# Sums of squares of the queries as rows in column tiles, turned to columns through DRAM

## The chip, the cores and the metric

The kernel runs on one core of a Trainium2 chip. A core has TensorE (PE) for matrix products, VectorE (DVE), ScalarE (ACT) and GpSimd (POOL) for elementwise work, SyncE (SP) that here only issues DMAs, and sixteen DMA engines. Each engine takes its instructions from its own queue in order, and semaphores connect the queues. The metric is the device time of one execution in microseconds.

## The reference

One layer of a streaming encoder is computed for 256 prompt rows and 64 sample rows together, so 320 time steps. After a projection, queries and keys are normalised per head, attention runs over bands of chunks, a gating part runs beside it, both are projected back, and a feed-forward part follows. What matters here is the normalisation of the queries:

```python
def rmsnorm(x, g):
    xf = x.astype(jnp.float32)
    y = xf * lax.rsqrt(jnp.mean(xf * xf, axis=-1, keepdims=True) + EPS)
    return (y * g.astype(jnp.float32)).astype(x.dtype)

z = rmsnorm(x, ln_g) @ w_in
q = z[..., :ATTN_WIDTH].reshape(*lead, N_KV_HEADS, GQA_GROUP, HEAD_DIM)
...
return rmsnorm(q, q_g), rmsnorm(k, k_g), v, zs
...
s = jnp.einsum('...qhgd,...khd->...hgqk', q, k).astype(jnp.float32) * (HEAD_DIM ** -0.5) + bias
```

There are 16 query heads of 64 values. For each head and time step one number is needed, the reciprocal root of the sum of 64 squares. It does not have to be multiplied into the query; it can be applied to the row of scores that the query gives.

## The kernel before, in words

Activations lie transposed: features on the 128 partitions, the 320 time steps along the free axis. Two heads fill the 128 partitions of one feature tile. A projection (`product`, `products`) makes 256 output features at a time, from 16 contraction tiles in four pieces of four. Each piece loads 512 KB of weights (`w_raw`, issued by SP), splits them into a high part on ACT (`w_hi`, line 115) and a low part on DVE (`w_lo`, line 116), three buffers of each, and PE runs 24 matmuls on them: high by high, high by low, low by high for eight products (line 141). All projections of the program follow one another on PE like this. Small work is put between pieces by `between_pieces`; its PE instructions go directly behind the last matmul of that piece.

The queries are made in four groups g of four heads (two feature tiles a, two heads p in each). `evict_q` scales a group, stores it in `qT` as [feature, block b of 64 steps, tile, step], and ACT squares it into `qsq`. `norm_q` (from line 316) then sums the squares. It uses the squares themselves as the stationary operand: for each of five blocks, 128 columns (two tiles of 64 steps) against `hone`, two columns of ones over the upper and lower 64 partitions. So the result stands as columns: partition = tile and step, two numbers per block, ten per group. DVE adds the epsilon (`r_q`, line 324) and GpSimd raises to the power -0.5 (`rq`, line 325). `rq` is read in `scores` (line 426) as a per-partition scalar when DVE takes a unit's scores out of PSUM.

The four calls stand behind pieces: group 0 in the first piece of the third query projection, group 1 in its third, group 2 in the second piece of the fourth projection, group 3 in the third piece of the first projection of v. Attention unit 0 (`attend(0)`, whose score matmuls are line 415) follows group 2; units 0 to 4 read `rq` of groups 0 and 1, units 5 to 9 that of groups 2 and 3. The scores also need `kzv`, the keys laid out in two halves, which DVE fills and two DMAs on GpSimd's queue complete (lines 371 and 372). The order within each engine's queue is set by the framework's scheduler, from the program's order and an estimate of times.

Of the kernel before, what the change touches and what calls it, by code (L numbers as in the profile page):

```python
# [8 lines left out]
F32 = mybir.dt.float32  # L9
F32R = mybir.dt.float32r  # L10
I32 = mybir.dt.int32
AF = mybir.ActivationFunctionType
ALU = mybir.AluOpType
AX = mybir.AxisListType

P = 128
T = 320
# [6 lines left out]
EPS = 1e-6  # L24
GELU_A = 0.044715
GELU_S = 0.7978845608028654
HD = 64
# [3 lines left out]
def hymba_step_kernel(ctx: ExitStack, tc: tile.TileContext, i, o):  # L31
    nc = tc.nc

    const = ctx.enter_context(tc.tile_pool(name="const", bufs=1))
    actp = ctx.enter_context(tc.tile_pool(name="actp", bufs=2))
    wp = ctx.enter_context(tc.tile_pool(name="wp", bufs=3))
    sm = ctx.enter_context(tc.tile_pool(name="sm", bufs=2))
    phase1 = ExitStack()
    at = phase1.enter_context(tc.tile_pool(name="at", bufs=2))
    dram = ctx.enter_context(tc.tile_pool(name="dram", bufs=1, space=bass.MemoryType.DRAM))  # L40
# [34 lines left out]

    ident = const.tile([P, P], F32, name="ident")
    make_identity(nc, ident)
    nhalf = const.tile([P, 16], F32, name="nhalf")
    nc.vector.memset(nhalf, -0.5)
    warm = const.tile([P, 1], F32, name="warm")  # L80
    nc.scalar.activation(out=warm, in_=nhalf[:, 0:1], func=AF.Exp)
# [12 lines left out]
    nc.gpsimd.memset(mean_hd.bitcast(F32), 0.0)  # L94
    for h in range(2):
        nc.gpsimd.memset(mean_hd[h * HD:(h + 1) * HD, h * HD:(h + 1) * HD].bitcast(F32), 1.0 / HD)
    hone = const.tile([P, 2], F32, name="hone")
    nc.vector.memset(hone, 0.0)
    nc.vector.memset(hone[0:HD, 0:1], 1.0)
    nc.vector.memset(hone[HD:P, 1:2], 1.0)  # L100
# [196 lines left out]
        nc.scalar.activation(out=kv, in_=kv_ps[:, :, 0:T], func=AF.Copy)  # L297
    rk, rx = rstd_b("rk"), rstd_b("rx")

    rq = at.tile([P, 4, 10], F32, name="rq", bufs=1)  # L300

    def evict_q(g, q_ps):
        qg = qT[:, :, 2 * g:2 * g + 2]
# [10 lines left out]
        nc.scalar.activation(out=sq, in_=qg, func=AF.Square)  # L314
        return sq

    def norm_q(g, sq):
        st = misc()
        for b in range(5):
            mm = nc.tensor.matmul(out=st[:, 2 * b:2 * b + 2], lhsT=sq[:, b].rearrange("p a t -> p (a t)"), rhs=hone,  # L320
                                  start=True, stop=True)
        narrow.append(mm.ins)
        r = at.tile([P, 10], F32, name="r_q", tag="r_q")
        nc.vector.tensor_scalar(out=r, in0=st[:, 0:10], scalar1=HD * EPS, scalar2=None, op0=ALU.add)
        nc.gpsimd.tensor_tensor(out=rq[:, g], in0=r, in1=nhalf[:, 0:10], op=ALU.pow)

# [27 lines left out]
    q0_sq = evict_q(0, q0_ps)  # L356
    q0_out = rests[-1]
    q1_sq = []

    def first_norms():  # L360
        rstd(ksq, mean_hd, EPS, rk)
        norm_q(0, q0_sq)
        q1_sq.append(evict_q(1, q1_ps))

    def keys():
        for dst, c in ((kn[:, 0:256], slice(0, 256)), (kn[:, 384:448], slice(256, 320))):
            nc.vector.scalar_tensor_tensor(out=dst, in0=zk[:, c], scalar=g_k, in1=rk[:, c], op0=ALU.mult, op1=ALU.mult)
        for h in range(2):
            hs = slice(h * HD, (h + 1) * HD)
            nc.vector.tensor_scalar(out=kz[hs, h], in0=kn[hs], scalar1=g_q[hs], scalar2=None, op0=ALU.mult)  # L370
        nc.gpsimd.dma_start(out=kz[HD:P, 0], in_=kz[0:HD, 0])
        nc.gpsimd.dma_start(out=kz[0:HD, 1], in_=kz[HD:P, 1])
        nc.gpsimd.dma_start(out=o["kpT"], in_=kn[:, 128:256])
        nc.gpsimd.dma_start(out=o["ksT"], in_=kn[:, 384:448])
        nc.gpsimd.dma_start(out=o["vpT"], in_=vT[:, 128:256])
        nc.gpsimd.dma_start(out=o["vsT"], in_=vT[:, 256:320])
        norm_q(1, q1_sq[0])
        values(0, 1)

    q2_ps = product(w_in, 0, KT, 512, xh, xl,  # L380
                    between_pieces={0: first_norms, 2: keys, 3: lambda: values(2, 3, 4, 5)},
                    halves_behind={1: lambda: q0_out})
    q2_sq = evict_q(2, q2_ps)

# [21 lines left out]
    def scores(u):  # L406
        blk_, kv = units[u]
        q0, k0, nk, b0 = blocks[blk_][0:4]
        js = slice(2 * kv, 2 * kv + 2)
        s_ps = [score_bank(p) for p in range(2)]  # L410
        for j in range(2):
            a = 2 * (2 * kv + j)
            for p in range(2):
                hs = slice(p * HD, (p + 1) * HD)
                mm = nc.tensor.matmul(out=s_ps[p][:, j * nk:(j + 1) * nk],  # L415
                                      lhsT=qT[hs, blk_, a:a + 2].rearrange("p a t -> p (a t)"),
                                      rhs=kz[hs, kv, k0:k0 + nk], start=True, stop=True)
        last = mm
        s = at.tile([P, 2, 2, 192], F32, name="s", tag="s", bufs=2)

        sv = s[:, :, :, 0:nk] if nk > HD else \
            s.rearrange("x p j k -> x p (j k)")[:, :, P:2 * P].rearrange("x p (j k) -> x p j k", j=2)
        for p in range(2):
            for j in range(2):
                c = 2 * blk_ + p
                nc.vector.scalar_tensor_tensor(out=sv[:, p, j], in0=s_ps[p][:, j * nk:(j + 1) * nk],
                                               scalar=rq[:, 2 * kv + j, c:c + 1],
                                               in1=bias[:, p, 2 * kv + j, b0:b0 + nk], op0=ALU.mult, op1=ALU.add)
        m = at.tile([P, 2, 2], F32, name="m", tag="m")
        nc.vector.tensor_reduce(out=m, in_=sv, axis=AX.X, op=ALU.max)  # L430
        sk = sinks_pj[:, :, js]
        nc.vector.tensor_tensor(out=m, in0=m, in1=sk, op=ALU.max)
        nm = at.tile([P, 2, 2], F32, name="nm", tag="nm")
        nc.vector.tensor_scalar(out=nm, in0=m, scalar1=-1.0, scalar2=None, op0=ALU.mult)
        es = at.tile([P, 2, 2], F32, name="es", tag="es")
        nc.vector.tensor_tensor(out=es, in0=sk, in1=m, op=ALU.subtract)
        nc.scalar.activation(out=es, in_=es, func=AF.Exp)
        den = at.tile([P, 2, 2], F32, name="den", tag="den")
        for p in range(2):
            for j in range(2):  # L440
                nc.scalar.activation(out=sv[:, p, j], in_=sv[:, p, j], func=AF.Exp, bias=nm[:, p, j:j + 1],
                                     accum_out=den[:, p, j:j + 1])
        nc.vector.tensor_tensor(out=den, in0=den, in1=es, op=ALU.add)
        nc.vector.reciprocal(out=den, in_=den)
        nc.gpsimd.tensor_tensor(out=sv, in0=sv,
                                in1=den[:, :, :, None].to_broadcast([P, 2, 2, nk]), op=ALU.mult)
        probs[u] = s
        return last

    def attend(i):  # L450
# [34 lines left out]
        if t is not None:  # L485
            for p in range(2):
                c = slice(min(x for _, x in cols) * P, (max(x for _, x in cols) + 1) * P)
                nc.vector.tensor_copy(out=pts[t % 2][p][:, c], in_=bank[p][:, c])

    q3_ps = product(w_in, 0, KT, 768, xh, xl,  # L490
                    between_pieces={1: lambda: (norm_q(2, q2_sq), attend(0)), 3: lambda: attend(1)})
    q3_sq = evict_q(3, q3_ps)

    def add_square(acc, src, first):
# [24 lines left out]
    acc_v = sums_rows("acc_v")  # L519
    for g in range(4):  # L520
        v_ps = product(w_in, 0, KT, 2304 + g * 256, xh, xl, between_pieces={
            1: lambda: attend(2 * g + 2), 2: lambda: norm_q(3, q3_sq) if g == 0 else None,
            3: lambda: attend(2 * g + 3)})
        gelu2(v_ps, gv[:, 2 * g:2 * g + 2])
        for a in range(2 * g, 2 * g + 2):
            add_square(acc_v, gv[:, a], a == 0)
            nc.gpsimd.tensor_scalar(out=gv[:, a], in0=gv[:, a], scalar1=g_sv[:, a:a + 1], scalar2=None, op0=ALU.mult)
# [195 lines left out]
```

## Time and profile before

| what | value |
|---|---|
| median of 3 runs | 1246.65 us (1246.59 to 1246.72) |
| span of the profiled execution | 1245.0 us |
| PE busy | 1240.9 us |
| DVE, ACT, POOL busy | 656.2, 491.3, 97.3 us |
| granted TensorE clock | 1.000 |
| DMA, mean | 151 GB/s |

The profiled execution's own time outside the profiler is not recorded; its span, first to last instruction, is 1.65 us below the median. In timeline rows the columns are start, length, engine, line, operation, output and inputs by the program's names, the tile of the array that a matmul uses (rows*columns), shape, and count of merged instructions; a bracket gives idle time before and what ended it. A plain fp32 matmul appears as two records, one for each pass.

### The profile page before, as it was taken

How to read it: one execution, taken by the hardware profiler on the slowest of the kernel's cores; microseconds unless marked ns; L12 is line 12 of the kernel's file. 1: busy time of each engine (PE TensorE's matmuls, PEld its weight loads, DVE VectorE, ACT ScalarE, POOL GpSimd, SP SyncE). 2: the span in 40 equal slices, each digit the busy share in tenths (PEclk: the TensorE clock that was granted, in tenths of full speed). 3: DMA queues.
4: the chain of work that ended last, by engine and by line, in shares of the span. 5: the costliest groups of instructions: out<-in, count | busy, mean ns of one | idle time of the engine just before them, and what ended most of it. 6: DMA issues, size and time to landing. Idle time of an engine off the chain costs nothing.

```text
span 1245.0 us, 20317 instructions
## 1 busy us (share of the span) xinstructions
PE 1240.9 (100%) x8560; PEld 1231.7 (99%) x8560; DVE 656.2 (53%) x787; ACT 491.3 (39%) x651; POOL 97.3 (8%) x89
## 2 busy tenths in 40 slices
PE   9999999999999999999999999999999999999998
PEld 9999999999999999999999999999999999999998
DVE  7777775987864444334454434444443344444343
ACT  7435655424543333333343333333333223433321
POOL 1134462201200000000000000000000000000000
PEclk9999999999999999999999999999999999999999
DMA  9744344544444444444444444445444444545540
GB/s 281 211 140 119 106 118 146 189 146 152 151 148 146 150 151 152 153 148 147 148 150 152 153 153 143 149 149 152 153 153 150 142 149 152 153 152 163 168 164 33
DMA packets 186988, 187.86 MB, mean 151 GB/s; under 512 B 6656, under 2 KB 186432, under 8 KB 186896
## 3 DMA queue, kind: packets, MB, share of 16 engines
q1 hardware_dynamic: 186096, 185.38, 48.0%
q8 instruction: 67, 1.10, 0.4%
q0 software_dynamic: 368, 0.93, 0.2%
q10 hardware_dynamic: 432, 0.24, 0.1%
q14 instruction: 25, 0.20, 0.0%
HBM read 182.98 MB, written 3.32 MB: 150 GB/s over the span
## 4 chain that ended last, share of the span: by engine, by line
PE 100%; DVE 0%; DVEq 0%; issue 0%
PE acc L141 93%; PE q_ps L237 1%; PE acc L237 1%; PE misc L141 1%; PE s_ps L415 1%; PE misc L465 0%; PE misc L472 0%; PE misc L320 0%; PE misc L84 0%; PE misc L538 0%; PE misc L477 0%; PE g_ps L551 0%; PE misc L551 0%; PE misc L186 0%; PE misc L187 0%; PE g_ps L553 0%
## 5 line engine op out<-in xcount | busy, mean ns | idle before, releaser
L116 DVE TENSOR_TENSOR w_lo<-w_raw,w_hi 128x1024 fp32r<-128x1024 f32 x332 | 413.3, 1245 | 430.5 <-ACT w_hi L115 422.0
L115 ACT ACTIVATE w_hi<-w_raw 128x1024 fp32r<-128x1024 f32 x332 | 351.8, 1060 | 697.6 <-PE acc L141 660.3
L141 PE MATMUL acc<-H2H,w_hi 128*128 128x320 f32 x1024 | 316.4, 309 | 0.0
L141 PE MATMUL acc<-H2L,w_hi 128*128 128x320 f32 x1024 | 316.4, 309 | 0.0
L141 PE MATMUL acc<-H2H,w_lo 128*128 128x320 f32 x1024 | 316.4, 309 | 0.0
L141 PE MATMUL acc<-FH,w_hi 128*128 128x320 f32 x992 | 306.5, 309 | 0.0
L141 PE MATMUL acc<-FL,w_hi 128*128 128x320 f32 x992 | 306.5, 309 | 0.0
L141 PE MATMUL acc<-FH,w_lo 128*128 128x320 f32 x992 | 306.5, 309 | 0.0
L141 PEld LDWEIGHTS acc<-H2H,w_lo 128*128 128x128 f32 x1024 | 192.2, 188 | 0.0
L141 PEld LDWEIGHTS acc<-H2H,w_hi 128*128 128x128 f32 x1024 | 192.2, 188 | 0.0
L141 PEld LDWEIGHTS acc<-H2L,w_hi 128*128 128x128 f32 x1024 | 192.2, 188 | 0.0
L141 PEld LDWEIGHTS acc<-FH,w_hi 128*128 128x128 f32 x992 | 186.2, 188 | 0.0
L141 PEld LDWEIGHTS acc<-FL,w_hi 128*128 128x128 f32 x992 | 186.2, 188 | 0.0
L141 PEld LDWEIGHTS acc<-FH,w_lo 128*128 128x128 f32 x992 | 186.2, 188 | 0.0
L141 PE MATMUL acc<-XH,w_hi 128*128 128x320 f32 x352 | 110.8, 315 | 0.0
L141 PE MATMUL acc<-XH,w_lo 128*128 128x320 f32 x352 | 108.8, 309 | 0.0
L141 PE MATMUL acc<-XL,w_hi 128*128 128x320 f32 x352 | 108.7, 309 | 0.0
L141 PEld LDWEIGHTS acc<-XH,w_hi 128*128 128x128 f32 x352 | 66.1, 188 | 2.1 <-issue 1.2
L141 PEld LDWEIGHTS acc<-XL,w_hi 128*128 128x128 f32 x352 | 66.1, 188 | 0.0
L141 PEld LDWEIGHTS acc<-XH,w_lo 128*128 128x128 f32 x352 | 66.1, 188 | 0.0
L639 DVE SCALAR_TENSOR_TENSOR tf<-acc,r 128x640 f32<-128x640 f32 x32 | 26.4, 825 | 41.9 <-PE acc L141 41.8
L654 DVE TENSOR_TENSOR xT<-xT,acc 128x640 f32<-128x640 f32 x31 | 25.5, 821 | 41.8 <-PE acc L141 41.8
(221 smaller groups left out, 1060.5 us busy)
## 6 DMA issues: line engine op xcount, KB each, us to landing
w_raw<-in_w_up SPq DMA_DIRECT2D x128, 512.0 KB
w_raw<-in_w_down SPq DMA_DIRECT2D x128, 512.0 KB
w_raw<-in_w_in SPq DMA_DIRECT2D x44, 512.0 KB
w_raw<-in_w_out SPq DMA_DIRECT2D x32, 512.0 KB
w_first<-in_w_in SPq DMA_DIRECT2D x14, 256.0 KB
out_yT<-xT SPq DMA_DIRECT2D x7, 320.0 KB
xT<-in_xT SPq DMA_DIRECT2D x8, 160.0 KB
xT<-in_xT SPq DMA_DIRECT2D x4, 320.0 KB
```

What stands on the lines that cost most here:

```text
L115: return (pin(nc.scalar.activation(out=hi, in_=raw, func=AF.Copy)).ins, pin(nc.vector.tensor_tensor(out=lo, in0=raw, in1=hi.bitcast(F32), ...
L116: pin(nc.vector.tensor_tensor(out=lo, in0=raw, in1=hi.bitcast(F32), op=ALU.subtract)).ins)
L141: mm = nc.tensor.matmul(out=out, lhsT=w_[:, k, g * P:(g + 1) * P], rhs=r_(kk), start=(kk == 0 and x == 0), stop=(kk == nk - 1 and x == 2))
L237: mm = nc.tensor.matmul(out=ps[:, 0:T], lhsT=w_[:, j, k, g * P:(g + 1) * P], rhs=r_(a + k), start=(a + k == 0 and x == 0), stop=(a + k == ...
L415: mm = nc.tensor.matmul(out=s_ps[p][:, j * nk:(j + 1) * nk], lhsT=qT[hs, blk_, a:a + 2].rearrange("p a t -> p (a t)"), rhs=kz[hs, kv, k0:k ...
L639: nc.vector.scalar_tensor_tensor(out=t, in0=ps[:, :, 0:T], scalar=0.0, in1=r2[:, None, :].to_broadcast([P, 2, T]), op0=ALU.max, op1=ALU.mult)
L654: nc.vector.tensor_tensor(out=xT[:, a, c], in0=xT[:, a, c], in1=p, op=ALU.add)
```

## The change

`norm_q` now takes two groups at once. The stationary operand is `hone`, widened to 32 columns with ones in the first two and zeros in the rest, and the squares stream past it: for each of four feature tiles c (two groups, two tiles) one fp32 matmul of 320 columns writes 32 partitions of one PSUM bank, from partition 32c on. Two rows of each 32 carry sums. ACT copies the bank to SBUF (`q_rows`), four DMAs on GpSimd's queue write the two rows of each tile into a DRAM tensor `q_dram`, and two DMAs read them back so that 64 time steps stand on partitions, with 20 numbers each (two heads, two groups, five blocks). DVE adds the epsilon in place, GpSimd takes the power of 20 columns. `scores` finds its column through `r_at`. The first call moves behind the second piece of the third query projection and covers groups 0 and 1; the second replaces the call of group 3 and covers groups 2 and 3.

```diff
-    nhalf = const.tile([P, 16], F32, name="nhalf")
+    nhalf = const.tile([P, 20], F32, name="nhalf")
...
-    hone = const.tile([P, 2], F32, name="hone")
+    hone = const.tile([P, 32], F32, name="hone")
...
-    rq = at.tile([P, 4, 10], F32, name="rq", bufs=1)
+    rq = at.tile([P, 40], F32, name="rq", bufs=1)
...
-    def norm_q(g, sq):
+    q_dram = dram.tile([2, 2, 2, 2, T], F32, name="q_dram")
+    r_at = lambda g, b, p: (g // 2) * 20 + p * 10 + (g % 2) * 5 + b
+
+    def norm_q(h, sqs):
+
         st = misc()
-        for b in range(5):
-            mm = nc.tensor.matmul(out=st[:, 2 * b:2 * b + 2], lhsT=sq[:, b].rearrange("p a t -> p (a t)"), rhs=hone,
-                                  start=True, stop=True)
+        for c in range(4):
+            mm = nc.tensor.matmul(out=st[c * 32:(c + 1) * 32, 0:T], lhsT=hone, rhs=sqs[c // 2][:, :, c % 2], start=True, stop=True)
         narrow.append(mm.ins)
-        r = at.tile([P, 10], F32, name="r_q", tag="r_q")
-        nc.vector.tensor_scalar(out=r, in0=st[:, 0:10], scalar1=HD * EPS, scalar2=None, op0=ALU.add)
-        nc.gpsimd.tensor_tensor(out=rq[:, g], in0=r, in1=nhalf[:, 0:10], op=ALU.pow)
+        rows = sm.tile([P, T], F32, name="q_rows", tag="w1", bufs=3)
+        nc.scalar.activation(out=rows, in_=st[:, 0:T], func=AF.Copy)
+        for c in range(4):
+            nc.gpsimd.dma_start(out=q_dram[h, c % 2, :, c // 2], in_=rows[c * 32:c * 32 + 2])
+        r = at.tile([P, 20], F32, name="r_q", tag="r_q")
+        for a in range(2):
+            nc.gpsimd.dma_start(out=r[a * HD:(a + 1) * HD],
+                                in_=q_dram[h, a].rearrange("p g (b t) -> t p (g b)", t=HD))
+        nc.vector.tensor_scalar(out=r, in0=r, scalar1=HD * EPS, scalar2=None, op0=ALU.add)
+        nc.gpsimd.tensor_tensor(out=rq[:, 20 * h:20 * h + 20], in0=r, in1=nhalf, op=ALU.pow)
...
     def first_norms():
         rstd(ksq, mean_hd, EPS, rk)
-        norm_q(0, q0_sq)
         q1_sq.append(evict_q(1, q1_ps))
...
-        norm_q(1, q1_sq[0])
         values(0, 1)
...
-                    between_pieces={0: first_norms, 2: keys, 3: lambda: values(2, 3, 4, 5)},
+                    between_pieces={0: first_norms, 1: lambda: norm_q(0, (q0_sq, q1_sq[0])), 2: keys, 3: lambda: values(2, 3, 4, 5)},
...
-                    between_pieces={1: lambda: (norm_q(2, q2_sq), attend(0)), 3: lambda: attend(1)})
+                    between_pieces={1: lambda: attend(0), 3: lambda: attend(1)})
...
-            1: lambda: attend(2 * g + 2), 2: lambda: norm_q(3, q3_sq) if g == 0 else None,
+            1: lambda: attend(2 * g + 2), 2: lambda: norm_q(1, (q2_sq, q3_sq)) if g == 0 else None,
```

The order of the queues, at the three places that the prediction speaks of. Line numbers after the change are 7 to 10 higher for the same statement. First PE in the third query projection. Before, at the end of its third piece, the call of group 1 and the first transposes of v (`vps`, line 340) behind it:

```order
L141 MATMUL acc<-XH,w_hi 128x320
L141 MATMUL acc<-XL,w_hi 128x320
L141 MATMUL acc<-XH,w_lo 128x320
L320 MATMUL misc<-hone,qsq 128x2 [waits DVE_49,Activation_49]
L320 MATMUL misc<-hone,qsq 128x2 x4
L340 MATMUL vps_785<-ident,kvx 128x128
L340 MATMUL misc<-ident,kvx 128x128 [waits DVE_49]
```

Of the change, at the end of the second piece, the call for groups 0 and 1:

```order
L141 MATMUL acc<-XH,w_hi 128x320
L141 MATMUL acc<-XL,w_hi 128x320
L141 MATMUL acc<-XH,w_lo 128x320
L324 MATMUL misc<-qsq,hone 32x320 x2
L324 MATMUL misc<-qsq,hone 32x320 [waits Activation_49]
L324 MATMUL misc<-qsq,hone 32x320
L141 MATMUL acc<-XH,w_hi 128x320
```

The five matmuls with two columns are gone here and at three other places, and four with 320 columns stand here and at one other.

GpSimd's queue during the third and fourth query projections, before: the stores of v, two powers, the stores of k, the two copies that complete `kzv`, the power of group 2.

```order
L375 DMA out_vpT<-kvx 128x128 [waits DVE_49]
L376 DMA out_vsT<-kvx 128x64
L325 TENSOR_TENSOR rq<-r_q,nhalf 128x10 [waits DVE_49,Pool_49]
L325 TENSOR_TENSOR rq<-r_q,nhalf 128x10 [waits DVE_49]
L373 DMA out_kpT<-kvx 128x128 [waits DVE_49]
L374 DMA out_ksT<-kvx 128x64 [waits DVE_49]
L371 DMA kzv<-kzv 64x448 [waits DVE_49]
L372 DMA kzv<-kzv 64x448 [waits DVE_49]
L325 TENSOR_TENSOR rq<-r_q,nhalf 128x10 [waits DVE_49]
```

Of the change:

```order
L384 DMA out_vpT<-kvx 128x128 [waits DVE_49]
L385 DMA out_vsT<-kvx 128x64
L329 DMA q_dram<-q_rows 2x320 [waits Activation_49]
L329 DMA q_dram<-q_rows 2x320 x3
L332 DMA r_q<-q_dram 64x20x1 [waits DMASW5_49,DMASW3_49]
L332 DMA r_q<-q_dram 64x20x1 [waits DMASW6_49,DMASW4_49,DMASW0_49]
L382 DMA out_kpT<-kvx 128x128 [waits DMASW1_49,DVE_49]
L383 DMA out_ksT<-kvx 128x64 [waits DMASW2_49,DVE_49]
L380 DMA kzv<-kzv 64x448 [waits DVE_49]
L381 DMA kzv<-kzv 64x448 [waits DVE_49]
L335 TENSOR_TENSOR rq<-r_q,nhalf 128x20 [waits DMASW0_49,DMASW7_49,DVE_49,Pool_49]
```

The six DMAs of the new trip stand ahead of the copies into `kzv`, and the power has moved behind them.

DVE's queue ahead of the first scores, before:

```order
L116 TENSOR_TENSOR w_lo<-w_raw,w_hi 128x1024 [waits DMAHW2_49,Activation_49]
L116 TENSOR_TENSOR w_lo<-w_raw,w_hi 128x1024 [waits DMAHW3_49,PE_49,Activation_49]
L324 TENSOR_SCALAR r_q<-misc 128x10 [waits PE_49,Pool_49]
L116 TENSOR_TENSOR w_lo<-w_raw,w_hi 128x1024 [waits DMAHW4_49,Activation_49]
L426 SCALAR_TENSOR_TENSOR s<-s_ps_911,rq,bias 128x64 [waits PE_49]
L426 SCALAR_TENSOR_TENSOR s<-s_ps_911,rq,bias 128x64 [waits Pool_49]
```

Of the change:

```order
L116 TENSOR_TENSOR w_lo<-w_raw,w_hi 128x1024 [waits DMAHW2_49,Activation_49]
L334 TENSOR_SCALAR r_q<-r_q 128x20 [waits DMASW7_49,DMASW0_49]
L116 TENSOR_TENSOR w_lo<-w_raw,w_hi 128x1024 [waits DMAHW3_49,PE_49,Activation_49]
L433 SCALAR_TENSOR_TENSOR s<-s_ps_901,rq,bias 128x64 [waits PE_49,Pool_49]
L433 SCALAR_TENSOR_TENSOR s<-s_ps_901,rq,bias 128x64
L433 SCALAR_TENSOR_TENSOR s<-s_ps_902,rq,bias 128x64 [waits PE_49]
L433 SCALAR_TENSOR_TENSOR s<-s_ps_902,rq,bias 128x64
L116 TENSOR_TENSOR w_lo<-w_raw,w_hi 128x1024 [waits DMAHW4_49,Activation_49]
```

The add of the epsilon now waits for DMAs instead of PE, and the weight split of `DMAHW4` stands behind the scores.

More of the change, by code (lines that the diff above doesn't have):

```diff
@@ L424, in scores @@
             for j in range(2):
-                c = 2 * blk_ + p
                 nc.vector.scalar_tensor_tensor(out=sv[:, p, j], in0=s_ps[p][:, j * nk:(j + 1) * nk],
-                                               scalar=rq[:, 2 * kv + j, c:c + 1],
+                                               scalar=rq[:, r_at(2 * kv + j, blk_, p):r_at(2 * kv + j, blk_, p) + 1],
                                                in1=bias[:, p, 2 * kv + j, b0:b0 + nk], op0=ALU.mult, op1=ALU.add)
```

## The prediction

> **What bounds the kernel now.** I read the page's busy shares first, then the chain of waits, then the timeline of TensorE around the four places where the change removes matmuls.
>
> ```profile
> span 1245.0 us, 20317 instructions
> PE 1240.9 (100%) x8560; PEld 1231.7 (99%) x8560; DVE 656.2 (53%) x787; ACT 491.3 (39%) x651; POOL 97.3 (8%) x89
> ...
> PE 100%; DVE 0%; DVEq 0%; issue 0%
> ...
> L141 PE MATMUL acc<-XH,w_lo 128*128 128x320 f32 x352 | 108.8, 309 | 0.0
> ```
>
> TensorE (PE) is busy for the whole span, the chain that ends last is PE alone, and the projection matmuls of L141 never wait. So the change is worth what it takes off PE's queue, less any wait it puts there. A matmul's duration (309 ns) is no price, since matmuls overlap; the distance between starts is. What L320 costs is read from starts, rows of PE's timeline:
>
> ```profile
> 52.74 1.17 PE L320 MATMUL misc<-hone,qsq 128*128 128x2 f32 x10
> 53.77 0.39 PE L141 MATMUL acc<-XH,w_hi 128*128 128x320 f32 x1
> 54.00 0.31 PE L141 MATMUL acc<-XL,w_hi 128*128 128x320 f32 x1
> 54.15 0.31 PE L141 MATMUL acc<-XH,w_lo 128*128 128x320 f32 x1
> ...
> 61.04 1.17 PE L320 MATMUL misc<-hone,qsq 128*128 128x2 f32 x10
> 62.07 0.31 PE L340 MATMUL vps<-ident,kvx 128*128 128x128 f32 x1
> ...
> 73.45 1.17 PE L320 MATMUL misc<-hone,qsq 128*128 128x2 f32 x10
> 74.55 0.66 PE L415 MATMUL s_ps<-kzv,qT 64*128 64x64 f32 x8
> ...
> 94.94 1.17 PE L320 MATMUL misc<-hone,qsq 128*128 128x2 f32 x10
> 95.98 0.39 PE L141 MATMUL acc<-XH,w_hi 128*128 128x320 f32 x1
> 96.21 0.31 PE L141 MATMUL acc<-XL,w_hi 128*128 128x320 f32 x1
> ```
>
> Five fp32 matmuls show as ten records: each runs as two passes. L141's normal step is 54.15 - 54.00 = 0.15 us.
>
> **Removed from PE.** First place: the second L141 starts 54.00 - 52.74 = 1.26 us after the first L320 record, where it would be one step after: 1.11 us. Fourth place: 96.21 - 94.94 - 0.15 = 1.12. Second place: the transpose comes 62.07 - 61.04 = 1.03 us late. Third place: 74.55 - 73.45 = 1.10, but L415 directly behind L141 starts 0.24 us after it instead of 0.15 (rows below), so 1.01. Sum: 4.27 us.
>
> **Added to PE.** Two groups of four fp32 matmuls on 128x32 column tiles, 320 columns each. No 128x32 tile runs in this trace; the nearest rows are other tiled fp32 matmuls.
>
> ```profile
> 82.14 0.31 PE L141 MATMUL acc<-XH,w_lo 128*128 128x320 f32 x1
> 82.38 0.71 PE L415 MATMUL s_ps<-kzv,qT 64*128 64x128 f32 x8
> ...
> 83.27 0.30 PE L141 MATMUL acc<-XL,w_hi 128*128 128x320 f32 x1
> ...
> 90.47 0.92 PE L415 MATMUL s_ps<-kzv,qT 64*128 64x192 f32 x8
> ...
> 182.74 0.33 PE L472 MATMUL s_ps<-pt,kzv 128*64 128x128 f32 x2
> ...
> 183.33 0.34 PE L477 MATMUL s_ps<-pt,kzv 64*64 64x128 f32 x4
> ```
>
> The last two rows show what runs together. The two column tiles of L472 cover 0.33 us where one record takes about that alone; the four 64x64 tiles of L477 cover 0.34 us. So one pass of all tiles goes as one round, then the second pass as another. L415 has pairs, hence four rounds; 192 columns take 0.92 - 0.71 = 0.21 us longer than 128, or 0.053 a round, 0.82 ns a column. A round of 128 is then about 0.11 us and one of 320 about 0.27. The isolated L415 block costs 83.27 - 82.14 - 2 x 0.15 = 0.83 us, of which four rounds are 0.44, so leaving and re-entering full-array work costs 0.39. My price for one new group: 2 x 0.27 + 0.39 = 0.93 us, for both 1.86. Bounds: below, two bare rounds (0.54 each group, 1.1 in all); above, eight serial passes plus the change of tiling (2.16 + 0.39, 5.1 in all). I take 0.93 because L477 is the nearest row in the number of tiles; what it does not show is four tiles that each read all 128 partitions.
>
> [...]
>
> PE's account is -4.27 + 1.86 = -2.4 us. The small norm product L187 only moves ahead of twelve L141s and costs its one step in either place.
>
> **What must not become a wait.** ScalarE gains two copies of 128x320 out of PSUM, VectorE's four 128x10 adds become two of 128x20, and GpSimd's four powers become two; both have gaps there. New is a trip through DRAM on GpSimd's queue: per group four writes of two rows, then two reads, each of 64 partitions by 20 values. Neighbouring values of a source row go to different partitions, so a read is 1280 runs of four bytes. Behind the reads in the first group stand the stores of k and both copies into kzv, and the scores on PE (L415) wait for the first of these copies.
>
> ```profile
> 17.83 0.79 POOL L251 DMA_DIRECT2D b_dram<-b_row  x1 [14.67 <-DVE b_row L249]
> 62.50 2.87 POOL L325 TENSOR_TENSOR rq<-r_q,nhalf 128x10 f32<-128x10 f32 x1 [5.33 <-DVE r_q L324]
> 66.01 0.61 POOL L373 DMA_DIRECT2D out_kpT<-kvx  x1 [0.64 <-DVE kvx L367]
> 66.61 0.54 POOL L374 DMA_DIRECT2D out_ksT<-kvx  x1
> 67.14 0.56 POOL L371 DMA_DIRECT2D kzv<-kzv  x1
> ...
> 179.46 0.88 POOL L171 TENSOR_TENSOR rs_rows<-r_rows,nhalf 128x3 f32<-128x3 f32 x1 [1.91 <-DVE r_rows L169]
> ...
> kzv<-kzv POOLq DMA_DIRECT2D x2, 112.0 KB, 2.3
> out_ksT<-kvx POOLq DMA_DIRECT2D x1, 32.0 KB, 1.7
> ...
> q1 hardware_dynamic: 186096, 185.38, 48.0%
> ```
>
> Issuing a DMA holds GpSimd 0.61 us for 128 runs (out_kpT) and 0.79 for 240 (b_dram): 1.6 ns a run, so 0.61 + 1152 x 0.0016 = 2.5 us for a read. Bounds: 0.55 us, if runs do not count, and 10.8 us, if all 0.54 us of the 64 runs of out_ksT belong to the runs (8.4 ns x 1280). Far apart; I take 2.5, the only slope the trace has.
>
> Now the clock of the first group. The new matmuls come one piece of 24 steps after L187: 52.74 + 0.15 + 3.5 = 56.4, done by 57.4. ScalarE's w_hi, freed by that piece, goes first (1.06 us), then the copy, to about 58.1. Four writes at 0.55 us keep GpSimd to 60.3; the third lands at 59.2 + 1.7 = 60.9 and lets the first read go. Two reads of 2.5 us end at 65.9, the two stores at 67.1, and the first kzv copy lands 2.3 us later, 69.4. PE wants it at 74.55 - 1.11 - 1.03 + 0.93 - 1.01 = 72.3. Cover: 2.9 us, and it is gone when a read takes over 3.9 us, 3 ns a run. The moving of the runs is no problem at 51 ns a packet (48.0% of 16 x 1245 us over 186096 packets of queue 1, and those are 1 KB): 80 runs per engine and read, 160 in all, is 8.2 us from 60.9, 69.1.
>
> The other cover is VectorE's. There the add on r now stands between two weight splits, ahead of the scores, and waits for the second read's landing, about 65.9 + 1.75 = 67.7.
>
> ```profile
> 71.12 1.23 DVE L116 TENSOR_TENSOR w_lo<-w_raw,w_hi 128x1024 fp32r<-128x1024 f32 x1 [0.52 <-ACT w_hi L115]
> ...
> 73.55 1.06 ACT L115 ACTIVATE w_hi<-w_raw 128x1024 fp32r<-128x1024 f32 x1 [2.46 <-PE acc L141]
> ...
> 75.98 0.85 DVE L426 SCALAR_TENSOR_TENSOR s<-s_ps,rq,bias 128x64 f32<-128x64 f32 x4
> ```
>
> PE is 1.2 us earlier by then (1.11 + 1.03 - 0.93), so VectorE is at that place near 71.12 - 1.2 = 69.9, and the read is in time. The power of 20 columns is 5.7 us by the line through 0.88 (3) and 2.87 (10): from about 70 to 75.7, where VectorE would otherwise reach the scores near 74 (75.98 less 2.2): some 2 us of waiting, and behind it the next w_lo, whose w_hi is made when a piece frees one of three buffers (73.55) and which PE reads two pieces, 7 us, later. So 2 us are covered; with the split's own place after the scores, some 3 more would be, and beyond that PE waits for weights. The second group has a softmax product and GELU work of GpSimd between its DMAs, and its r is first used in the fifth score unit:
>
> ```profile
> 103.14 1.58 POOL L509 TENSOR_TENSOR gc<-gc,z 128x640 f32<-128x640 f32 x1 [2.44 <-DVE gc L508]
> ...
> 109.55 0.18 DVE L444 RECIPROCAL den<-den 128x4 f32<-128x4 f32 x1
> ...
> 117.81 0.82 PE L465 MATMUL misc<-ident,s 128*128 128x128 f32 x6
> ```
>
> Everything 2 us earlier: GELU product done at 102.7, reads to 107.7, landed at 109.5, while VectorE reaches its add after the reciprocal at 107.6. It waits 2 us; the transposes of that unit start 8 us after the reciprocal, and the weight split behind has two pieces. No PE wait.
>
> **The rivals.** (A) The DMA runs cost more. At 5 ns a run, between my slope and the upper bound, a read takes 0.6 + 1152 x 0.005 = 6.4 us; the first kzv copy lands at 60.9 + 12.8 + 1.15 + 2.3 = 77.2, PE stands still at L415 for 4.9 us, and the result is 1246.65 - 2.4 + 4.9 = 1249.1, slower. It decides from 3 ns a run; at the upper bound it is 1258. For it: no row has four-byte runs. Against: the only slope is half of that. [...] (B) Four column tiles that read all partitions go only two at a time, as in L472: four rounds, 4 x 0.27 + 0.39 = 1.47 per group, gain 4.27 - 2.94 = 1.3 us, 1245.3. For it: two at a time is all that is shown with 128 rows. Against: L477 has four starting together. (C) No overlap at all, the tiles do not do what they are there for: 5.1 us added, 1247.5. (D) Re-entry is cheaper than at L415 (half, 0.2): 2 x 0.74 added, gain 2.8, 1243.9.
>
> **How the numbers follow.** The sum is made on the profiled execution, span 1245.0; the three timed runs have a median of 1246.65, 1.65 us above it, and I take the difference as unchanged. Forecast: 1246.65 - 2.4 = 1244.25, called 1244.3, chance 0.52, its own spread 1243.9 to 1244.8. (A) 0.17, (B) 0.15, (C) 0.04, (D) 0.12. About 0.2%, 2.5 us, is what a measurement of this kernel can tell from no change, so the bound is 1244.16 and the forecast lies at its edge: of its 0.52 I put 0.18 below it. With (D): faster 0.30. Slower is (A) less the part of it where the wait only eats the gain: 0.14. Same: 0.56. The range 1243.6 to 1248.3 leaves out the long tail of (A) and little below (D).
>
> **What would show each step.** L324 as eight records in two rounds 0.27 us apart, each of four starts within 0.03 us, and the second L141 behind it 0.9 us late; eight starts 0.27 apart is (C), four is (B). GpSimd's two reads near 2.5 us each and kzv issued before 68. L415 on PE at 72.3 without a gap before it; a gap that a kzv landing ends is (A). VectorE waiting some 2 us at the first scores, and not before. If PE shows a wait between 57 and 120 us at any other place, my account of the covers is wrong; if the four L320 groups were worth less than 4.27 us, the gain is.

## The result, and the profile after

| | before | after |
|---|---|---|
| median | 1246.62 us (16 runs, 1246.0 to 1247.5) | 1244.45 us (16 runs, 1243.15 to 1245.16) |
| span of the profiled execution | 1245.0 us | 1242.7 us |

The ratio is 0.9981, with a 95% interval of 0.9974 to 0.9987: 2.2 us less. The forecast was 1244.3.

The page of the changed kernel, its first lines and the chain of waits:

```profile
span 1242.7 us, 20289 instructions
PE 1238.3 (100%) x8536; PEld 1227.0 (99%) x8536; DVE 658.5 (53%) x785; ACT 492.3 (40%) x653; POOL 102.5 (8%) x99
...
PE 97%; DMA 2%; SPq 1%; issue 0%; ACT 0%; DVE 0%; DVEq 0%; ACTq 0%
```

PE is still busy from end to end. The chain shows 2% of DMA where it showed none, all of it between 4 and 36 us of the span, while the input and the first weights arrive and ahead of the change's first block at 56.9 us. The list of what PE waited for has only two entries, L84 for 0.8 us and L186 for 0.3, and the change touches neither place. The timeline of PE around the two new blocks (start, length, engine, line, operation, output and inputs, tile of the array, shape, merged records):

```profile
56.68 0.31 PE L141 MATMUL acc<-XH,w_lo 128*128 128x320 f32 x1
56.92 0.75 PE L324 MATMUL misc<-qsq,hone 128*32 128x320 f32 x8
57.59 0.42 PE L141 MATMUL acc<-XH,w_hi 128*128 128x320 f32 x1
57.85 0.31 PE L141 MATMUL acc<-XL,w_hi 128*128 128x320 f32 x1
...
72.52 0.66 PE L423 MATMUL s_ps<-kzv,qT 64*128 64x64 f32 x8
...
93.01 0.75 PE L324 MATMUL misc<-qsq,hone 128*32 128x320 f32 x8
```

A block's cost is the distance from the L141 ahead of it to the second L141 behind it, less two steps of 0.147 us. The first is 57.85 - 56.68 - 0.29 = 0.88 us; the second, by its neighbours at 92.77 and 93.93, 0.87. Together 1.75 us were added. Taken one by one, the first four of the eight records of the first block start within 0.02 us of each other from 56.92 on, 7 ns apart, and the other four in the same way from 57.21 on: two rounds 0.29 us apart, and in each all four tiles together. The scores at 72.52 carry no bracket, so they did not wait.

The same kind of difference around the four places of L320 in the trace of before gives 1.12, 1.07, 1.01 and 1.12, so 4.31 us removed. At the second place, which L320 shared with two transposes, this is the joint block of 1.29 us less the 0.22 that the transposes take alone after the change. The four transposes one piece further on also became 0.13 us cheaper; in both traces no L320 stands beside them, and why is not shown. PE's account is therefore -4.31 - 0.13 + 1.75 = -2.7 us. The profiled span fell by 2.3 us; the rest is not the change's. L186, ahead of all of it, began at 53.02 us, and at 52.59 in the execution of before; over the profiles of all kernels here that start varies by 0.9 us. In the first repeat below it began 0.1 us after that of before, and its span is 2.7 us shorter.

What became of the trip through DRAM, on GpSimd (a bracket is idle time ahead, and what ended it):

```profile
58.55 2.03 POOL L329 DMA_DIRECT2D q_dram<-q_rows  x4 [8.53 <-ACT q_rows L327]
64.11 1.83 POOL L332 DMA_DIRECT2D r_q<-q_dram  x2 [3.54 <-DMA q_dram<-q_rows]
...
67.04 0.56 POOL L380 DMA_DIRECT2D kzv<-kzv  x1
...
70.39 4.45 POOL L335 TENSOR_TENSOR rq<-r_q,nhalf 128x20 f32<-128x20 f32 x1 [2.26 <-DVE r_q L334]
```

on VectorE:

```profile
70.07 0.18 DVE L334 TENSOR_SCALAR r_q<-r_q 128x20 f32<-128x20 f32 x1 [0.31 <-DMA r_q<-q_dram]
...
74.87 0.86 DVE L433 SCALAR_TENSOR_TENSOR s<-s_ps,rq,bias 128x64 f32<-128x64 f32 x4 [3.46 <-POOL rq L335]
```

and in the list of DMA issues (count, KB each, median us from issue to landing):

```profile
kzv<-kzv POOLq DMA_DIRECT2D x2, 112.0 KB, 3.5
...
q_dram<-q_rows POOLq DMA_DIRECT2D x8, 2.5 KB, 2.0
...
r_q<-q_dram POOLq DMA_DIRECT2D x4, 5.0 KB, 4.1
```

The line view of the writes (L329) adds how long the slowest took:

```profile
L329 POOL DMA_DIRECT2D q_dram<-q_rows x8: 497/509/613, 58.5 to 99.6; - x8
...
DMA to landing us min/median/max: 1.5/2.0/4.0
```

A read holds GpSimd 0.92 us, half of the 1.83 for two. The copy into kzv is issued at 67.04 and lands 3.5 us later (the median of the two copies), at 70.5, some 2 us before the scores. VectorE stands 3.5 us at the first scores, from 71.4 us on: to 73.2 PE's scores were not done either, and the last 1.7 us are for GpSimd's power alone. PE shows nothing of it. In the second group the add waits 0.56 us and the power takes 4.07.

### The profile page after: what moved, and what is told of

Same layout as the page of the kernel before. It is cut to its first block, busy times and chain, and to the rows that moved or that the text cites. A ratio compares the mean times of both kernels' runs of the same rounds, so it can differ in the third digit from the quotient of the medians.

```text
span 1242.7 us, 20289 instructions
## 1 busy us (share of the span) xinstructions
PE 1238.3 (100%) x8536; PEld 1227.0 (99%) x8536; DVE 658.5 (53%) x785; ACT 492.3 (40%) x653; POOL 102.5 (8%) x99
## 4 chain that ended last, share of the span: by engine, by line
PE 97%; DMA 2%; SPq 1%; issue 0%; ACT 0%; DVE 0%; DVEq 0%; ACTq 0%
PE acc L141 93%; DMA w_first<-in_w_in 1%; PE misc L141 1%; SPq L110 1%; PE s_ps L423 1%; PE misc L472 0%; DMA w_raw<-in_w_in 0%; DMA xT<-in_xT 0%; PE misc L479 0%; PE misc L545 0%; PE misc L484 0%; PE g_ps L558 0%; PE misc L558 0%; PE misc L324 0%; PE misc L187 0%
## 5 line engine op out<-in xcount | busy, mean ns | idle before, releaser
L141 PE MATMUL acc<-H2H,w_hi 128*128 128x320 f32 x1024 | 316.7, 309 | 0.0
L141 PE MATMUL acc<-H2H,w_lo 128*128 128x320 f32 x1024 | 316.7, 309 | 0.0
L141 PE MATMUL acc<-H2L,w_hi 128*128 128x320 f32 x1024 | 316.7, 309 | 0.0
L141 PE MATMUL acc<-FH,w_hi 128*128 128x320 f32 x992 | 306.8, 309 | 0.0
L141 PE MATMUL acc<-FH,w_lo 128*128 128x320 f32 x992 | 306.8, 309 | 0.0
L141 PE MATMUL acc<-FL,w_hi 128*128 128x320 f32 x992 | 306.8, 309 | 0.0
L141 PEld LDWEIGHTS acc<-H2H,w_lo 128*128 128x128 f32 x1024 | 192.3, 188 | 0.0
L141 PEld LDWEIGHTS acc<-H2L,w_hi 128*128 128x128 f32 x1024 | 192.3, 188 | 0.0
L141 PEld LDWEIGHTS acc<-H2H,w_hi 128*128 128x128 f32 x1024 | 192.3, 188 | 0.0
L141 PEld LDWEIGHTS acc<-FH,w_lo 128*128 128x128 f32 x992 | 186.3, 188 | 0.0
L141 PEld LDWEIGHTS acc<-FH,w_hi 128*128 128x128 f32 x992 | 186.3, 188 | 0.0
L141 PEld LDWEIGHTS acc<-FL,w_hi 128*128 128x128 f32 x992 | 186.3, 188 | 0.0
L141 PE MATMUL acc<-XH,w_hi 128*128 128x320 f32 x352 | 111.0, 315 | 0.0
L141 PE MATMUL acc<-XH,w_lo 128*128 128x320 f32 x352 | 108.8, 309 | 0.0
L141 PE MATMUL acc<-XL,w_hi 128*128 128x320 f32 x352 | 108.8, 309 | 0.0
L141 PEld LDWEIGHTS acc<-XH,w_hi 128*128 128x128 f32 x352 | 66.1, 188 | 3.1 <-issue 2.5
L141 PEld LDWEIGHTS acc<-XL,w_hi 128*128 128x128 f32 x352 | 66.2, 188 | 0.0
L141 PEld LDWEIGHTS acc<-XH,w_lo 128*128 128x128 f32 x352 | 66.1, 188 | 0.0
```

Of the source, the lines that this page charges most:

```text
L141: mm = nc.tensor.matmul(out=out, lhsT=w_[:, k, g * P:(g + 1) * P], rhs=r_(kk), start=(kk == 0 and x == 0), stop=(kk == nk - 1 and x == 2))
```

## The experiments

### The change again, and its three alternatives on PE

Theory: the gain is the price of the blocks on PE. Four tiles run together; it is neither the number of calls nor their place. Four kernels ran on one chip; the kernel before has a median of 1246.54 us there (33 runs). First the changed kernel as it stands.

> The change itself, as control on this chip. Theory A (the gain is PE steps: 4.3 us of column-sum matmuls removed, 1.75 us of tiled matmuls added, the trip through DRAM hidden): about 2.3 us under the kernel before (ratio 0.998). Rival B (the gain is not these matmuls but where the work now stands, or one call instead of two): the same time.

1244.09 us, ratio 0.9980 [0.9972, 0.9989], span 1242.3. The result repeats.

Second, the old product at the new places: both groups in one call, one add, one power, and no trip through DRAM.

```diff
-        for c in range(4):
-            mm = nc.tensor.matmul(out=st[c * 32:(c + 1) * 32, 0:T], lhsT=hone, rhs=sqs[c // 2][:, :, c % 2], start=True, stop=True)
+        for g in range(2):
+            for b in range(5):
+                mm = nc.tensor.matmul(out=st[:, 10 * g + 2 * b:10 * g + 2 * b + 2],
+                                      lhsT=sqs[g][:, b].rearrange("p a t -> p (a t)"), rhs=hone, start=True, stop=True)
...
-        rows = sm.tile([P, T], F32, name="q_rows", tag="w1", bufs=3)
...
+        nc.vector.tensor_scalar(out=r, in0=st[:, 0:20], scalar1=HD * EPS, scalar2=None, op0=ALU.add)
```

> The old matmuls (five of two columns for each group, squares as stationary operand) at the new places, two groups in one call, one add and one power of 20 columns, no trip through DRAM. Theory A: PE pays two blocks of 20 records, 2.2 us each, about the old 4.3 us in all, so the time is that of the kernel before (within 0.4 us), 2.3 us over the change. Rival B: the time of the change.

1246.86 us, ratio 1.0003 [0.9994, 1.0012]: the whole gain is gone. PE's timeline of this kernel:

```profile
56.35 0.31 PE L141 MATMUL acc<-XH,w_lo 128*128 128x320 f32 x1
56.50 2.29 PE L323 MATMUL misc<-hone,qsq 128*128 128x2 f32 x20
...
58.88 0.31 PE L141 MATMUL acc<-XL,w_hi 128*128 128x320 f32 x1
```

The block costs 58.88 - 56.35 - 0.29 = 2.24 us, twice what a call of one group cost. So merging calls and moving them is worth nothing, and the trip through DRAM, which this kernel does not make, costs the changed kernel no time on PE: the two blocks differ by 2 x (2.24 - 0.88) = 2.7 us, and the medians of the two kernels by 2.8.

Third, the new product with the array whole: the ones are shifted within a stationary operand of 128 columns, and four matmuls add up in one bank.

```diff
-    hone = const.tile([P, 32], F32, name="hone")
+    hone = const.tile([P, 224], F32, name="hone")
...
-            mm = nc.tensor.matmul(out=st[c * 32:(c + 1) * 32, 0:T], lhsT=hone, rhs=sqs[c // 2][:, :, c % 2], start=True, stop=True)
+            mm = nc.tensor.matmul(out=st[:, 0:T], lhsT=hone[:, 96 - 32 * c:224 - 32 * c], rhs=sqs[c // 2][:, :, c % 2],
+                                  start=c == 0, stop=c == 3)
```

> The rows are summed on the whole array: stationary operand 128 wide with the ones in columns 32c and 32c+1, four matmuls accumulated into the same bank; all else as in the change. Theory A: no change of tiling (saves about 0.35 us a group), but eight passes of 0.27 us one after another, 2.2 us a group instead of 0.87: 2.7 us over the change, 0.4 us over the kernel before. Rival B: the time of the change.

1246.95 us, ratio 1.0001 [0.9992, 1.0010]. Its block in PE's timeline:

```profile
56.98 0.31 PE L141 MATMUL acc<-XH,w_lo 128*128 128x320 f32 x1
57.13 2.31 PE L324 MATMUL misc<-qsq,hone 128*128 128x320 f32 x8
...
59.42 0.31 PE L141 MATMUL acc<-XL,w_hi 128*128 128x320 f32 x1
```

59.42 - 56.98 - 0.29 = 2.15 us, eight passes of 0.27 each with no tile beside another. Streaming the squares past the ones is as dear as the old way as long as the passes go one after another. The difference of the two blocks, 2.15 - 0.88 = 1.27 us, is there twice, 2.5 us; the medians differ by 2.9. This is the share of the gain that comes from four tiles at once: all of it.

Fourth, every tile's matmul twice, which separates the price of a round from that of changing over to tiles.

```diff
-        for c in range(4):
+        for c in [0, 1, 2, 3] * 2:
             mm = nc.tensor.matmul(out=st[c * 32:(c + 1) * 32, 0:T], ...
```

> Each of the four tiled matmuls is issued twice (the second overwrites the same sums). Theory A, four tiles at once: two more rounds of 0.27 us a group, the block from 0.87 to 1.42 us, 1.1 us over the change. If the tiles ran one after another, eight more passes a group, 4.3 us over the change. Rival B: the time of the change.

1245.13 us, ratio 0.9989 [0.9980, 0.9998], 1.04 us over the repeat. PE's timeline:

```profile
57.04 0.31 PE L141 MATMUL acc<-XH,w_lo 128*128 128x320 f32 x1
57.28 1.28 PE L324 MATMUL misc<-qsq,hone 128*32 128x320 f32 x16
...
58.74 0.31 PE L141 MATMUL acc<-XL,w_hi 128*128 128x320 f32 x1
```

The block is 58.74 - 57.04 - 0.29 = 1.41 us, 0.53 more for two more rounds. A round is 0.27 us. What is left of 0.88 after two rounds is 0.34 us for leaving and re-entering the whole array. By its parts: the first tile starts 0.24 us after L141 instead of 0.15, and the two L141 behind the block start 0.36 and 0.25 us after their predecessors instead of 0.27 and 0.15; the rest is that a round's four starts are spread over 0.02 us.

### The reads' runs

Theory from the prediction: a read's issue is paid by its four-byte runs, 1.6 ns each. The reads now fetch whole runs of 20 values. This leaves out the turning of rows to columns, so the factors belong to other heads and steps; every instruction stays.

```diff
-                                in_=q_dram[h, a].rearrange("p g (b t) -> t p (g b)", t=HD))
+                                in_=q_dram[h, a].rearrange("p g t -> (p g t)").rearrange("(t n) -> t n", n=20))
```

> The reads take 20 values that lie next to each other for each partition, 64 runs of 80 bytes instead of 1280 of four; the turning to columns is left out with it, so the factors land at the wrong heads and steps. It measures what the runs cost. If 0.92 us of issue is 0.55 and 0.3 ns a run: 0.55 us a read; if runs cost nothing: still 0.92. Landing, 4.1 us in the change, nearer 2.5 if the runs make it, and unchanged if it is the queue. Theory A: the time of the change within 0.4 us, since nothing of it is on PE's path. Rival C too; a rival that the DRAM trip costs PE time through the weight loads expects a gain.

1244.08 us (10 runs), ratio 0.9979 [0.9970, 0.9988] against a kernel before of 1246.61: no difference to the changed kernel. The line view of the read, first of the changed kernel (ns min/median/max, first and last start):

```profile
L332 POOL DMA_DIRECT2D r_q<-q_dram x4: 902/922/976, 64.1 to 103.4; - x4
...
DMA to landing us min/median/max: 3.2/4.1/5.2
```

and of this one:

```profile
L332 POOL DMA_DIRECT2D r_q<-q_dram x4: 537/584/654, 63.6 to 102.5; - x4
...
DMA to landing us min/median/max: 1.8/2.7/3.6
```

1216 runs fewer save 0.34 us of issue, 0.28 ns a run, about a sixth of the slope that the prediction took from two other DMAs. They also save 1.4 us of landing (4.1 to 2.7). So the four-byte runs cost more in landing than in issue, and here that cost was covered.

### Where the cover ends

The prediction's rival on the other side, (A), was a kzv that lands late. More reads, into tiles that nothing uses, push kzv back on GpSimd's queue in the first group: eight at first, later two, four and six.

```diff
+        for x in range(8 if h == 0 else 0):
+            more = at.tile([P, 20], F32, name=f"r_more{x}", bufs=1)
+            nc.gpsimd.dma_start(out=more[0:HD], in_=q_dram[h, x % 2].rearrange("p g (b t) -> t p (g b)", t=HD))
```

> In the first group each of the two reads from DRAM is followed by four more like it into tiles that nothing uses, eight in all, ahead of the copies into kzv on GpSimd's queue. Theory A (the trip is hidden, with 2 us of cover: in the profile of the change kzv is issued at 67.0, lands 3.5 us later, and PE wants it at 72.5): eight reads at 0.92 us put kzv at 74.4 and its landing at 77.9, PE stands 5.4 us at the first scores, and the time is 5.4 us over the change, 3.1 us over the kernel before. Rival C (nothing near the scores waits for this queue, the cover is much larger): the time of the change.

1254.05 us, ratio 1.0062 [1.0047, 1.0077], span 1252.1. The loss against the changed kernel is about 10 us where 5.4 were expected. GpSimd:

```profile
73.57 0.58 POOL L383 DMA_DIRECT2D kzv<-kzv  x1
```

PE:

```profile
71.96 0.66 PE L426 MATMUL s_ps<-kzv,qT 64*128 64x64 f32 x4
79.52 1.11 PE L426 MATMUL s_ps<-kzv,qT 64*128 64x64 f32 x4 [6.91 <-DMA kzv<-kzv]
...
83.13 0.47 PE L141 MATMUL acc<-XH,w_hi 128*128 128x320 f32 x1
83.40 0.47 PE L141 MATMUL acc<-XL,w_hi 128*128 128x320 f32 x1
...
84.98 0.31 PE L141 MATMUL acc<-XL,w_hi 128*128 128x320 f32 x1
```

Two things were missing in the expectation. kzv landed 5.9 us after its issue instead of 3.5, behind all those reads, so the wait was 6.9 us. And after it L141 steps by 0.27 us (83.13 to 83.40) instead of 0.15, up to about 85. The view by stretches (start:end, length, busy time and count of PE, weight loads, VectorE, ScalarE, GpSimd; then the granted clock, the DMA share, GB/s) shows why:

```profile
74.60:74.80 0.20, 0.00 (x0) 0.00 (x0) 0.00 (x0) 0.00 (x0) 0.13 (x2) 0.78 0.91 205
...
84.80:85.00 0.20, 0.20 (x3) 0.20 (x2) 0.00 (x0) 0.00 (x0) 0.00 (x0) 0.62 0.00 0
```

Ahead of the first stretch the granted clock is 1.00 and behind the second again; between them it is 0.50. It is a half from 74.71 to 84.95 us (0.78 over 0.2 us means 0.088 us at a half; 0.62 means 0.152). Is that the price of any standstill, or only of a long one? And where does the cover end?

> Two more reads of the same 64x20 pieces into tiles that nothing uses, in the first group only, on GpSimd's queue ahead of kzv. In the changed kernel kzv is issued at 67.0 and lands 3.5 us later, and TensorE needs it 2.0 us after that. Each more read holds GpSimd 0.88 us (run with eight). Theory of a cover of 2.0 us: issue at 68.8, landing 3.5 to 4.1 us later, so the scores on TensorE wait 0 to 0.4 us and the time is 1244.1 to 1244.5. Rival, the cover was larger or smaller than the one profile shows: no wait and 1244.1 here and a wait of under 1 us with four reads, or a wait of over 1 us here, 1245.1 or more.

1244.04 us (10 runs), ratio 0.9980 [0.9970, 0.9989] against 1246.68. kzv is issued at 68.22, 1.2 us later than in the changed kernel, and lands at 71.1. PE waits for nothing there.

> Four more reads in the first group. Issue of kzv at 70.6; if its landing takes 3.5 us as in the changed kernel the scores wait 1.6 us, if it grows in proportion to the reads (5.9 us with eight, so 4.7) 2.8 us. Theory that only a long standstill takes the clock down: granted clock 1.00 in every stretch, time 1245.7 to 1246.9, no slower than before. Rival, that any standstill of this place costs more than its length (with eight reads 2 to 3 us beside 6.9 us of wait): stretches at 0.5 behind the wait and 1248 or more.

1248.58 us (10 runs, 1246.94 to 1250.20), ratio 1.0017 [1.0008, 1.0026]: about 2 us more than the wait explains, and the theory that only a long standstill takes the clock down has fallen. PE:

```profile
72.29 0.66 PE L426 MATMUL s_ps<-kzv,qT 64*128 64x64 f32 x4
74.86 1.11 PE L426 MATMUL s_ps<-kzv,qT 64*128 64x64 f32 x4 [1.92 <-DMA kzv<-kzv]
76.33 0.47 PE L141 MATMUL acc<-XL,w_hi 128*128 128x320 f32 x1
...
81.35 0.31 PE L141 MATMUL acc<-XH,w_lo 128*128 128x320 f32 x1
```

and the stretches in which its clock changes:

```profile
74.40:74.60 0.20, 0.00 (x0) 0.00 (x0) 0.20 (x1) 0.00 (x0) 0.20 (x1) 0.64 0.40 92
...
81.20:81.40 0.20, 0.20 (x3) 0.20 (x2) 0.00 (x0) 0.00 (x0) 0.00 (x0) 0.79 0.00 0
```

PE stood for only 1.92 us, and the clock went to a half 1.5 us into it, at 74.46, until 81.28. Against the kernel with two more reads this execution is 5.8 us longer: it came to the scores 0.3 us later, waited 1.92, lost 1.3 in the scores and the L141 behind them (72.29 to 76.33 is 4.04 us, against 0.85 without a wait), and 2.2 over the nineteen slow steps to 81.35 (5.02 us instead of 2.79). So 3.5 us went beyond the wait, nearly twice the wait. Not all of it is the clock's. PE worked at a half for 6.4 of the 6.83 us; half of that, 3.2 us, is an estimate of the loss by the clock (in the nineteen steps alone 2.2 of 5.02 us were lost). The rest, 0.3 us, fits what became of the scores: their eight records no longer run in pairs, since the four that do not need the late copy went ahead alone (x4 in 0.66 us in the rows above, where the changed kernel has x8 in 0.66). That makes eight rounds instead of four. The ten timed runs lie between 1246.94, at a mean clock of 1.000, and 1250.20, at 0.997: not every execution pays it.

> Six more reads. Issue of kzv at 72.3, landing 5.3 us later by proportion, so a wait of 5.1 us, near the 4.9 us that the prediction's slower rival named. If the wait alone counts, 1249.2, as the rival was priced. If TensorE's clock drops behind it as it did behind 6.9 us, 2 to 3 us more, 1251 to 1252, and the rival was priced too low.

1250.14 us (6 runs), ratio 1.0032 [1.0020, 1.0044]. PE waited 3.77 us, less than the 5.1 expected, because kzv landed in 4.7. The stretches:

```profile
76.80:77.00 0.20, 0.20 (x2) 0.20 (x3) 0.12 (x1) 0.00 (x0) 0.04 (x1) 0.98 1.11 358
...
80.40:80.60 0.20, 0.20 (x3) 0.20 (x3) 0.00 (x0) 0.18 (x2) 0.00 (x0) 0.98 0.00 0
```

The clock is a half from 76.99 to 80.41, that is, it went down 0.25 us after PE had started again. Reckoned as for four reads, 1.1 us were lost in the scores and the L141 behind them (72.31 to 78.01, less 0.85 and the wait) and 1.1 over nine slow steps, 2.2 together, less than with the shorter wait. For eight reads the same gives 1.3 and, over fifteen steps, 1.8. All four together:

| more reads | kzv issued | lands after, us | PE stood, us | clock at a half, us | lost beyond the wait, us | of it by the clock, us | median us |
|---|---|---|---|---|---|---|---|
| 2 | 68.22 | 2.9 | 0 | 0 | 0 | 0 | 1244.04 |
| 4 | 70.39 | 4.4 | 1.92 | 6.83 | 3.5 | 3.2 | 1248.58 |
| 6 | 72.00 | 4.7 | 3.77 | 3.41 | 2.2 | 1.7 | 1250.14 |
| 8 | 73.57 | 5.9 | 6.91 | 10.24 | 3.1 | 2.7 | 1254.05 |

The clock's part is the estimate above, half of the time at a half in which PE worked (with eight reads it stood for 4.81 of the 10.24 us). The three lengths at a half, 6.83, 3.41 and 10.24 us, are two, one and three times 3.41 us. The clock went down 1.5 us into the wait of 1.92 us and 2.1 us into that of 6.91; with the wait of 3.77 us it went down 4.0 us after the wait began, 0.25 us after its end. What sets these moments and lengths is not shown. With two more reads, where PE did not wait, the clock was 1.00 in every stretch from 65 to 95 us; in the profiled execution with four, a wait of 1.92 us was enough. No wait between these two was measured here.

The cover ends between two and four more reads, that is between 1.2 and 3.4 us of later issue, which agrees with the 2 us read from the trace; the landing changed as well, so these are bounds and no measurement.

### Two versions that might be better

The squares and the ones in fp32r, the type of the weights' two parts, with the whole array as in the third kernel. What the type does to the digits of the sums was not measured; each product is then one record in the trace (x4 below, where the third kernel has x8):

```diff
-    hone = const.tile([P, 32], F32, name="hone")
+    hone = const.tile([P, 224], F32R, name="hone")
...
-        sq = sm.tile([P, 5, 2, 64], F32, name="qsq", tag="w2", bufs=4)
+        sq = sm.tile([P, 5, 2, 64], F32R, name="qsq", tag="w2", bufs=4)
```

> Squares and ones in fp32r (the squares are rounded to it), summed on the whole array as in the full-width kernel: four single passes of 0.15 us, no change of tiling. Theory A: a block of 0.6 us instead of 0.87, 0.5 us under the change, 2.8 us under the kernel before. If the price of the full-width block was not its passes: 2.2 us a group as there, 2.7 us over the change.

1243.80 us (10 runs), ratio 0.9978 [0.9969, 0.9988]. PE:

```profile
56.32 0.31 PE L141 MATMUL acc<-XH,w_lo 128*128 128x320 f32 x1
56.47 0.74 PE L324 MATMUL misc<-qsq,hone 128*128 128x320 f32 x4
...
57.20 0.31 PE L141 MATMUL acc<-XL,w_hi 128*128 128x320 f32 x1
```

57.20 - 56.32 - 0.29 = 0.59 us, four steps of L141's kind with no change-over, 0.29 less than a tiled block, so 0.6 us for both. The median is 0.3 us under that of the repeat of the changed kernel, and the intervals do not tell the two apart.

Second, the second group's block directly behind the scores of the same piece, which are tiled too, so that one change-over serves both:

```diff
-            1: lambda: attend(2 * g + 2), 2: lambda: norm_q(1, (q2_sq, q3_sq)) if g == 0 else None,
+            1: lambda: (attend(2 * g + 2), norm_q(1, (q2_sq, q3_sq)) if g == 0 else None),
```

> The second group stands directly behind the scores of attention unit 2, one piece earlier, so tiled work follows tiled work of another shape. If the 0.33 us beside the rounds is paid once for leaving and re-entering the whole array: about 0.3 us under the change. If it is paid at each change of tile shape: 0.1 us or nothing. No wait elsewhere: its r comes earlier.

1244.85 us (11 runs), ratio 0.9985 [0.9976, 0.9994]. The joint block costs 1.95 us where the two cost 1.27 + 0.87 = 2.14, so 0.19 us is saved, between the 0.3 of one change-over for both and the 0.1 or nothing of one at each change of shape; but PE has a new wait, from the list of waits:

```profile
PE misc L472 <- POOL s L452: 0.9, 1, 0.9
```

GpSimd now reaches the softmax product of a later unit at 169.35 us instead of 166.28 in the repeat, since the scheduler put its work in another order. The small saving is lost there.

## Why the prediction was right, point by point

- **Removed from PE:** 4.27 us forecast, 4.31 measured by differences around the four places.
- **Added to PE:** 0.93 us a group forecast, 0.88 and 0.87 measured. The round was right at 0.27 (by the doubled kernel); the change-over was 0.34 instead of 0.39. So rivals (B), two tiles at a time, and (C), none, are out: the whole-array kernel shows what (C) would have cost but for the change-over, eight passes one after another. Nor was the change-over as low as (D) had it (0.2).
- **The trip through DRAM is hidden:** right, and that kzv's issue came out to 0.1 us is luck: two wrong terms cancelled. kzv was to be issued at 67.1 and was at 67.04. The prediction had let the first read go after 1.7 us of landing, at 60.9; the slowest write took up to 4.0 us and the read started at 64.11, 3.2 us later. Against that, two reads were to take 5.0 us and took 1.83, 3.2 us less, since a run costs 0.28 ns and not 1.6. The slope that failed came from two DMAs of different shape and size, in which the runs were not the only difference.
- **The cover:** 2.9 us forecast, 2.0 in the trace. The copy's landing was taken as 2.3 us from the trace of before; behind the reads it took 3.5.
- **VectorE:** the first add waited 0.3 us (none forecast, since the second read was to land at 67.7 and landed at 70.0), the scores 3.5 (2 forecast), the second add 0.6 (2 forecast). The power of 20 columns was 4.45 and 4.07 us, not 5.7, so it ended before the forecast 75.7, at 74.8. The wait is longer all the same because VectorE reached the scores at 71.4 and not near 74: the forecast took its arrival from the trace of before, where L324's wait of 2.4 us for PE and a weight split still stand ahead of the scores. None of this reached PE, as forecast: the weight split that waited behind the scores (75.64 in VectorE's timeline; PE reads it two pieces later) had its slack.
- **Rival (A):** its place was right and its price too low. The kernel with a wait of 3.8 us is 6.1 us over the one with two more reads and no wait (1250.14 against 1244.04). In its profile the granted clock was 0.50 for 3.41 us, from 0.25 us after the end of the wait on, and with the wait of 6.91 us for 10.24 us. By the rows with 3.77 and 6.91 us, its 4.9 us would have been nearer 1251 or 1252 than 1249.1 (an estimate).
- **The sum:** -2.4 us forecast, -2.7 by PE's account, -2.2 in the medians and -2.5 in the repeat. Both halves of the sum were a little pessimistic; that the first median came within 0.2 us of the forecast is in part luck, since the start of L186 alone differs by up to 0.9 us between profiles.

## What to carry to other kernels

When one engine is busy from end to end, price a change by the distance between starts around its block, not by durations: here it gave the gain to 0.3 us. Here the small products paid when they ran as tiles beside each other (0.88 us a block), and the change-over (0.34 us) should be shared among as many rounds as possible; the same fp32 product over the whole array gained nothing (2.15 us a block, 1246.95 us). In fp32r, where that type is allowed, the product over the whole array gained as much without tiles (0.59 us a block, 1243.80 us). More reads ahead of kzv on one queue delayed it twice, by their issue (from 67.0 to 73.6 us with eight) and by its longer landing (2.2 us before, 2.9 to 5.9 here), so check the cover by adding more of the same transfer until it breaks.

## What the runs showed of the hardware that was not expected

- With a wait of 1.92 us on TensorE its granted clock was 0.50 for 6.83 us; with one of 3.77 us for 3.41, with one of 6.91 us for 10.24. The price beyond the wait (3.5, 2.2 and 3.1 us) does not follow its length, and the time differs from run to run (1246.94 to 1250.20 us for one kernel).
- Four 128x32 tiles that each read all 128 partitions start 7 ns apart (changed kernel) and finish a round of 320 columns in 0.27 us (doubled kernel), as long as one pass over the whole array takes (third kernel).
- Four-byte runs cost 0.28 ns each in GpSimd's issue (0.92 against 0.58 us), and lengthen the landing from 2.7 to 4.1 us. Copies queued behind such reads land later than the 2.2 us of the kernel before: in 3.6 us behind the two reads of the changed kernel, and 2.9, 4.4, 4.7 and 5.9 with two, four, six and eight more.
